# The second product of an MLP, product by product over eight pairs of units, with the sums on VectorE and the squares on ScalarE

## The chip, the cores and the metric

One core of one Trainium2 chip runs the whole program. The metric is the device time of one execution in microseconds (us), lower is better; the median of several runs counts. The engines are named TensorE (PE; PEld is its weight load), VectorE (DVE), ScalarE (ACT), GpSimd (POOL) and SyncE (SP), which issues most transfers.

## The reference, cut to what matters

Two layers over 1024 latent tokens and 256 context tokens of width 1024; layer 0 mixes with windowed attention, layer 1 with gated linear attention. Behind each mixer stands an MLP with 4096 hidden units, in float32:

```python
def channel_mlp(h, w_in, w_out):
    return jnp.square(jax.nn.relu(h @ w_in)) @ w_out

x_lat = x_lat + m_lat[2] * rms_norm(y_lat, g_post_mix[i])
f_lat = channel_mlp(modulate(x_lat, g_pre_mlp[i], m_lat[3], m_lat[4]), w_mlp_in[i], w_mlp_out[i])
x_lat = x_lat + m_lat[5] * rms_norm(f_lat, g_post_mlp[i])
```

The context goes through layer 0's MLP as well and is dropped after layer 1's mixer. The output is the latent stream.

## The kernel before, in words

Tokens are handled in tiles of 128: tiles 0 and 1 are the context, 2 to 5 and 6 to 9 the two halves of the latent tokens. Every float32 product is made from three matmuls: each operand is split into a high part (a cast on ScalarE) and a low part (a subtract on VectorE; both in `split`, L207), and `mm3` (L225) adds high x high, high x low and low x high. Such a triple is the unit of TensorE's work here.

Both products of an MLP use seven products of sums instead of eight (Winograd's form of Strassen's scheme) on quarters: activations by halves of the tokens and of the features, weights by halves of the features and of the columns. The products are numbered 1 to 7 and run in the order 1, 6, 7, 4, 5, 3, 2. Products 1, 6, 7 and 4 run into one bank and 5 and 3 into another; in between, the bank is read and added to an accumulator.

The first product (`mlp_hidden`, L836) walks over 16 pairs of hidden units (a unit is 128 of the 4096). The sums of weight quarters are on GpSimd (L884). A bank goes through ScalarE (copy, rectify) and the square is a GpSimd product (`squared`, L886). The hidden units are stored in DRAM, in layer 0 with layer 1's modulation vectors computed alongside (`mod_sums`).

The second product (`mlp_out`, L981) walks over blocks of pairs of units: sizes 3, 3, 3, 3, 3 in layer 0 and 4, 4, 3, 3 in layer 1. In a block a product is made for one pair of tiles after the other (five pairs in layer 0, the first of them the context's; four in layer 1), with all units of the block in a row for each; then the bank is read (`read`, L997: ScalarE copies the first time, VectorE adds after that, L1004). The sums of weight quarters (L1035) and of hidden quarters (L1078) are on GpSimd. The units that are left, two in layer 0 and four in layer 1, are multiplied as they are, tile by tile (`last_block`, L1143, tile name `py`). There a finished tile goes to `finish`: in layer 0 (`finish0`, L1701) norm, gate (on GpSimd, L1717), residual, norm, transposed modulated input of layer 1, and layer 1's first projection (`gla_v`); in layer 1 (`finish1`, L1836) norm, gate, residual and the store of the output.

What is issued when stands on a written timeline: `tl.at(t, f)` gives each step a nominal time, and `run` issues in the order of these times. The framework then orders each engine's instructions, earlier issued first among those that it deems ready. Loads are issued on SyncE's queue, in order. All large buffers come from one pool of 45 slots of 128 x 1024 floats (`u`; `SLOTS`, L39); a load waits until a slot is free. TensorE's banks are four single ones (`ps1`, L203) and two double ones (`ps2`, L200). The context's products are in half of a double one (`half_bank`).

Of the kernel before, what the change touches and what calls it, by code (L numbers as in the profile page):

```python
# [18 lines left out]
P = 128  # L19
# [24 lines left out]
class Acts:  # L44
    """Activations with the features on the partitions, as high and low parts, by groups of token tiles."""
# [32 lines left out]
class Timeline:  # L78
    """What is to be issued, each at a time of its own on a nominal clock; run() issues in the order of these times."""
# [86 lines left out]
class Backbone:  # L166
    def __init__(self, es, tc, t, out):
        self.tc, self.nc, self.t, self.out = tc, tc.nc, t, out
        self.n = 0
        self.cp = es.enter_context(tc.tile_pool(name="cp", bufs=1))  # L170
# [31 lines left out]

    def ps1(self, s="b"):  # L203
        return self.pp.tile([P, 512], F32, tag="b", name=self.nm(s), bufs=4)

# [5 lines left out]
    def weight(self, srcs, s="w"):  # L211
        """Loads one 128 x 1024 unit of a weight and splits it into a high and a low part."""
# [19 lines left out]
    def rms(self, x, junk):  # L232
        """1 / rms(x), over the features."""
# [12 lines left out]
    def consts(self):  # L246
# [25 lines left out]
        # 32 columns from a feature tile's two on; what comes of the others is never read  # L272
# [45 lines left out]
    def mod_columns(self, l, j, acc):  # L318
        """Columns g * (1 + scale) or shift, for lat (s = 0) and ctx (s = 1)."""
# [3 lines left out]
        for s, a in enumerate(acc):  # L323
            col = out[:, s, :]
            for q in range(2):
                pt = self.ps1("modT")
# [13 lines left out]
    def mod_gate(self, l, which, acc):  # L340
        """gate * g_post, a stream's half of the columns on 32 partitions."""
# [4 lines left out]
        ps = self.ps1("mod")  # L346
# [14 lines left out]
    def mod_first(self):  # L361
        """Layer 0's first shift and scale, one feature tile after the other."""
# [41 lines left out]
    def gate_rows(self, l, which, s):  # L404
        """gate * g_post as a row over all partitions."""
# [3 lines left out]
        for j in range(2):  # L409
            r = 32 * (2 * s + j)  # L410
            pb = self.ps1("grow")
# [5 lines left out]
    def normed(self, x, junk=None):  # L417
        """x (128 tokens x 1024) over its rms; in place where there is another place for the squares."""
# [8 lines left out]
    def modulated(self, xn, l, which, s, dst=(), put=None):  # L427
        """The normed tile, transposed, modulated and split into the pieces of dst, or put where put says."""
        nc = self.nc
        G, S = self.pre[l, which]  # L430
        for q in range(2):
            pt = self.ps1("xt")
# [18 lines left out]
    def post_norm(self, y, x, grow):  # L451
        """x + gate * g_post * rms(y)."""
# [15 lines left out]
    def attn_consts(self):  # L468
# [6 lines left out]
        # by pairs of query heads: pair of kv heads, place within the group, kv head  # L475
# [4 lines left out]
        # keys: previous block | own block | next block | ctx  # L480
# [27 lines left out]
    def first_tiles(self, xs, h, pre):  # L508
        """Modulation, weights and projections of the first two tiles, by feature tile as the loads arrive."""
# [51 lines left out]
    def qkv_out(self, i, pq, pkv):  # L561
        """Rows of q, k and v; the rotary positions on latent tiles."""
# [14 lines left out]
    def keys(self, i):  # L577
        """Transposed keys of a tile as high and low parts, each twice over the partitions: in steps."""
# [36 lines left out]
    def queries(self, qs, i, g):  # L615
        """Transposed queries of a block, of eight heads: high parts on one half of the partitions, low on the other."""
# [48 lines left out]
    def block(self, i):  # L665
        """Keys of a block of 128 queries: latent range, width, mask and key tiles."""
# [11 lines left out]
    def scores(self, i, p, i4, qs):  # L678
        """Probabilities of a pair of query heads (one of each kv head of the pair p)."""
# [43 lines left out]
    def turned(self, i, probs):  # L723
        """The pair's probabilities with the keys on the partitions, by key tile and head."""
# [43 lines left out]
    def attention(self, steps, weights, o_ready):  # L768
        """Pairs of heads in turn: the turning of the probabilities lags the scores, and the values lag that."""
# [7 lines left out]
        for t in range(len(pairs) + LAG_T + 1):  # L777
# [12 lines left out]
            if t < len(pairs) and i4 == 0:  # L790
                # the next unit's queries, and the keys of the tile after the next, in the course of this unit
# [20 lines left out]
    def out_proj(self, o, wo, between):  # L812
        """y (128 tokens x 1024, in PSUM) = o @ w_o; between: what to issue in its midst."""
# [13 lines left out]
    def hidden_store(self, ctx):  # L827
        return [
            (
                self.dp.tile([P, 4, 2, P], F32, name=self.nm("hd")),  # L830
                self.dp.tile([P, 2, P], F32, name=self.nm("hc")) if ctx else None,
            )
            for _ in range(HID // P)
        ]

    def mlp_hidden(self, tl, t0, x, store, g):  # L836
        """Puts the squared rectified hidden units on the timeline, to be stored; the first g pairs of units side by side."""
# [48 lines left out]
        def squared(t, dst):  # L886
            nc.gpsimd.tensor_tensor(dst, t, t, op=ALU.mult)  # L887

        def out(m, a, half, t):
            s = st[m]  # L890
            if ("h", a) not in s:
                s["h", a] = self.u((P, 4, 2, P), s="h")
            squared(t.rearrange("p (i t) -> p i t", i=4), s["h", a][:, :, half, :])
# [1022 lines left out]
```

## Time and profile before

| what | value |
|---|---|
| median of 3 runs | 2704.67 us (2697.41 to 2709.02) |
| profiled execution: own time (its span) | 2705.4 us |
| TensorE matmuls busy | 2590.4 us, 96% |
| VectorE busy | 1881.2 us, 70% |
| GpSimd busy | 1234.1 us, 46% |
| ScalarE busy | 1184.8 us, 44% |
| transfers | 276.30 MB, mean 102 GB/s |

The span is what the profile covers, first instruction to last; nothing of the execution's time lies outside it here. A busy matmul is counted from its start to its modelled end, and matmuls overlap, so TensorE's share is not its share of the best pace. In the span, layer 0's first product runs from 638 us on, its second from 1070, the plain units from 1466; in layer 1 the second product runs from about 2354 to 2698.

### The profile page before, as it was taken

How to read it: one execution, taken by the hardware profiler on the slowest of the kernel's cores; microseconds unless marked ns; L12 is line 12 of the kernel's file. 1: busy time of each engine (PE TensorE's matmuls, PEld its weight loads, DVE VectorE, ACT ScalarE, POOL GpSimd, SP SyncE). 2: the span in 40 equal slices, each digit the busy share in tenths (PEclk: the TensorE clock that was granted, in tenths of full speed). 3: DMA queues.
4: the chain of work that ended last, by engine and by line, in shares of the span. 5: the costliest groups of instructions: out<-in, count | busy, mean ns of one | idle time of the engine just before them, and what ended most of it. 6: DMA issues, size and time to landing. Idle time of an engine off the chain costs nothing.

```text
span 2705.4 us, 36859 instructions
## 1 busy us (share of the span) xinstructions
PE 2590.4 (96%) x13562; PEld 2140.4 (79%) x13562; DVE 1881.2 (70%) x2650; ACT 1184.8 (44%) x2414; POOL 1234.1 (46%) x1287
## 2 busy tenths in 40 slices
PE   7999999998999999999999899999998999999998
PEld 5777888887778888777777788888786888777777
DVE  4788766657877565788996724736648555689886
ACT  3336777645333333533333634434445433454332
POOL 0355655314535456655562512212314656775741
PEclk9999999999999999999999999999999999999999
DMA  9311001321555555322122322002221333531313
GB/s 301 101 55 40 4 2 25 86 86 59 172 165 168 183 180 198 123 105 81 57 87 99 133 54 83 25 23 94 94 95 46 124 110 118 194 140 38 150 71 117
DMA packets 174998, 276.30 MB, mean 102 GB/s; under 512 B 18504, under 2 KB 117088, under 8 KB 174816
## 3 DMA queue, kind: packets, MB, share of 16 engines
q1 hardware_dynamic: 172224, 264.50, 30.0%
q0 software_dynamic: 2592, 9.44, 0.9%
q8 instruction: 107, 1.75, 0.3%
q14 instruction: 75, 0.61, 0.1%
HBM read 214.13 MB, written 59.77 MB: 101 GB/s over the span
## 4 chain that ended last, share of the span: by engine, by line
PE 71%; DVE 18%; issue 4%; ACT 3%; DMA 2%; POOL 2%; SPq 0%; DVEq 0%; POOLq 0%; ACTq 0%
PE p L228 4%; PE p L230 4%; PE p L229 4%; DVE h L209 4%; PE pa L229 3%; PE pa L230 3%; PE pa L228 3%; PE o L756 3%; DVE wu L209 3%; PE pt L737 3%; PE y L230 2%; PE y L228 2%; PE y L229 2%; DVE ma L310 2%; PE rp L230 2%
## 5 line engine op out<-in xcount | busy, mean ns | idle before, releaser
L228 PE MATMUL p<-wu,h 128*128 128x512 f32 x812 | 320.6, 395 | 12.1 <-DVE acc L1004 10.2
L229 PE MATMUL p<-wu,h 128*128 128x512 f32 x812 | 319.0, 393 | 2.8 <-DVE wu L209 2.8
L230 PE MATMUL p<-wu,h 128*128 128x512 f32 x812 | 318.0, 393 | 2.4 <-DVE h L209 2.4
L887 POOL TENSOR_TENSOR h<-s 128x512 f32<-128x512 f32 x128 | 159.7, 1251 | 205.8 <-ACT s L930 188.1
L241 POOL TENSOR_SCALAR rs<-ss 128x1 f32<-128x1 f32 (+1 forms) x81 | 29.3, 361 | 422.5 <-ACT later L235 271.7
L209 DVE TENSOR_TENSOR wi<-wi,wi 128x512 fp32r<-128x512 f32 x176 | 180.5, 1058 | 46.9 <-ACT wi L208 45.9
L310 DVE SCALAR_TENSOR_TENSOR ma<-wm,cT,ma 128x1024 f32<-128x1024 f32 x112 | 166.8, 1521 | 47.1 <-DMA wm<-in_w_mod 46.9
L228 PEld LDWEIGHTS p<-wu,h 128*128 128x128 f32 x812 | 153.8, 189 | 50.6 <-issue 6.2
L1004 DVE TENSOR_TENSOR acc<-acc,p 128x512 f32<-128x512 f32 x220 | 145.7, 678 | 65.6 <-PE p L230 65.4
L230 PEld LDWEIGHTS p<-wu,h 128*128 128x128 f32 x812 | 153.7, 189 | 37.0 <-DVE h L209 4.4
L229 PEld LDWEIGHTS p<-wu,h 128*128 128x128 f32 x812 | 153.8, 189 | 36.2 <-DVE wu L209 3.9
L209 DVE TENSOR_TENSOR wu<-wu,wu 128x512 fp32r<-128x512 f32 x145 | 148.3, 1023 | 13.2 <-ACT wu L208 13.2
L925 ACT COPY s<-pa 128x512 f32<-128x512 f32 x96 | 56.0, 585 | 226.5 <-PE pa L230 217.8
L209 DVE TENSOR_TENSOR h<-hr,h 128x512 fp32r<-128x512 f32 x145 | 150.3, 1037 | 6.5 <-ACT h L208 5.8
L208 ACT CAST h<-hr 128x512 fp32r<-128x512 f32 x145 | 89.9, 620 | 130.6 <-PE p L230 85.7
L704 DVE CUSTOM_DVE_ANT_0 pr<-sc,mask,nsink 128x640 f32<-128x640 f32 (+2 forms) x144 | 108.5, 775 | 42.9 <-PE sc L693 41.0
L721 POOL TENSOR_SCALAR pr<-pr,den 128x640 f32<-128x640 f32 (+2 forms) x160 | 117.7, 749 | 36.5 <-DVE den L719 17.1
L929 DVE TENSOR_TENSOR s<-pc,s 128x512 f32<-128x512 f32 x64 | 43.8, 685 | 125.5 <-ACT s L925 109.5
L709 ACT ACTIVATE pr<-pr,nm 128x640 f32<-128x640 f32 (+2 forms) x160 | 118.5, 742 | 28.2 <-DVE nm L704 25.0
L208 ACT CAST wu<-wu 128x512 fp32r<-128x512 f32 x145 | 89.9, 620 | 90.3 <-PE p L230 75.3
L208 ACT CAST wi<-wi 128x512 fp32r<-128x512 f32 x176 | 102.9, 616 | 49.1 <-DVE ma L310 16.8
L1078 POOL TENSOR_TENSOR hr<-hr 128x512 f32<-128x512 f32 x29 | 40.9, 1423 | 180.2 <-DMA hr<-hd 159.2
(395 smaller groups left out, 7878.6 us busy)
## 6 DMA issues: line engine op xcount, KB each, us to landing
wm<-in_w_mod SPq DMA_DIRECT2D x96, 512.0 KB, 4.7
wi<-in_w_mlp_in SPq DMA_DIRECT2D x64, 512.0 KB, 5.3
hd<-h SPq DMA_DIRECT2D x64, 512.0 KB, 3.3
wu<-in_w_mlp_out SPq DMA_DIRECT2D x64, 512.0 KB, 5.0
hr<-hd SPq DMA_DIRECT2D x64, 512.0 KB, 7.3
x<-in_x SPq DMA_DIRECT2D x16, 512.0 KB, 3.6
wgr<-in_gla_w_in SPq DMA_DIRECT2D x16, 512.0 KB, 4.2
x1d<-xo POOLq DMA_DIRECT2D x10, 512.0 KB, 3.3
```

The costliest lines, as they stand in the source:

```text
L208: self.nc.scalar.copy(hi, src)
L209: self.nc.vector.tensor_tensor(lo, src, hi.bitcast(F32), op=ALU.subtract)
L228: mm(out, a[0], b[0], start=start, stop=False, skip_group_check=onto)
L229: mm(out, a[0], b[1], start=False, stop=False, skip_group_check=onto)
L230: mm(out, a[1], b[0], start=False, stop=stop, skip_group_check=onto)
L310: nc.vector.scalar_tensor_tensor(acc[s], raw, c, acc[s], ALU.mult, ALU.add)
L704: nc.vector.tensor_tensor_reduce(out=like(pr), in0=like(ps[e][:, off:768]), in1=mask, scale=1.0, scalar=self.nsink[:, c0 + e : c0 + e + 1] ...
L709: nc.scalar.activation(pr, pr, AF.Exp, bias=nm[:, e : e + 1], scale=-1.0, accum_out=sums[:, e : e + 1])
L721: nc.gpsimd.tensor_scalar(probs[e], probs[e], den[:, e : e + 1], 0.0, ALU.mult, ALU.add)
L737: nc.tensor.transpose(pt[:, P * j : P * (j + 1)], probs[e][:, P * kt : P * (kt + 1)], self.ident)
L887: nc.gpsimd.tensor_tensor(dst, t, t, op=ALU.mult)
L1004: nc.vector.tensor_add(acc[i][:, cs], acc[i][:, cs], bank)
```

## The change

The second product has two halves of eight pairs of units. In a half, each of the seven products is made unit by unit: for unit pair j, one triple for every pair of tiles, then the next j. So all banks of a product fill at once, and each is read once per product and half. All 32 units go through the seven products; `last_block` is gone. For each product and unit the quarter of the hidden units and that of the weight are loaded side by side into one slot, summed there by VectorE where the product needs sums, and split as one 128 x 1024 operand. The hidden units are stored by halves of the tokens, and the context's by quarters. Nothing of it is on GpSimd but the small steps of the norms. In the first product the square is a ScalarE activation. Layer 0's tiles 1 and 6 to 9 are finished while products 3 and 2 of the second half run, tiles 0 and 2 to 5 at the end; the gate's product is on VectorE. In layer 1, tiles 6 to 9 are finished during product 3, and tiles 2 to 5 by halves of the columns. `split_last` makes the last 4 (5) units of product 2 run pair of tiles by pair of tiles. While `tight` is set, single-bank helpers take a double bank, since all four single ones hold sums.

The diff, without lines that only drop comments:

```diff
+    def bank(self, s):
+        return self.half_bank(s) if self.tight else self.ps1(s)
...
         def squared(t, dst):
-            nc.gpsimd.tensor_tensor(dst, t, t, op=ALU.mult)
+            nc.scalar.activation(dst, t, AF.Square)
...
-    def mlp_out(self, tl, t0, l, pairs, sizes, store, finish, halved=False):
+    def mlp_out(self, tl, t0, l, pairs, store, split_last, done):
...
+        mm = 0.68
+        step = mm * np_
+        order = (1, 6, 7, 4, 5, 3, 2)
+        when, t = {}, t0
+        for kh in range(2):
+            for k in order:
+                for j in range(8):
+                    when[kh, k, j] = t
+                    t += step
...
+        def fetch(kh, k, j):
+            m = 8 * kh + j
+            if k == 6:
+                k3[m], raw[k, m] = unit("k3"), unit("wh")
+                hid(k3[m][:, 0, :], m, 21)
+                wgt(k3[m][:, 1, :], m, 12)
+                hid(raw[k, m][:, 0, :], m, 22)
+                wgt(raw[k, m][:, 1, :], m, 22)
+                return
+            hq, wq = {1: (11, 11), 4: (22, 21), 5: (11, 22), 3: (12, 22), 2: (12, 21)}[k]
+            r = unit("k2" if k == 1 else "wh")
+            hid(r[:, 0, :], m, hq)
+            wgt(r[:, 1, :], m, wq)
...
+        def sums(kh, k, j):
+            m = 8 * kh + j
+            tt = nc.vector.tensor_tensor
+            if k == 6:
+                a, b, r = k2[m], k3[m], raw.pop((k, m))
+                tt(b[:, 0, :], a[:, 0, :], b[:, 0, :], op=ALU.subtract)
+                tt(b[:, 1, :], r[:, 1, :], b[:, 1, :], op=ALU.subtract)
+                tt(a[:, 0, :], r[:, 0, :], b[:, 0, :], op=ALU.subtract)
+                tt(a[:, 1, :], b[:, 1, :], a[:, 1, :], op=ALU.add)
+                return
+            a, r = k2[m], raw[k, m]
+            if k in (4, 5):
+                tt(r[:, 1, :], r[:, 1, :], a[:, 1, :], op=ALU.subtract)
+            if k == 5:
+                tt(r[:, 0, :], a[:, 0, :], r[:, 0, :], op=ALU.add)
+            if k == 3:
+                tt(r[:, 0, :], r[:, 0, :], a[:, 0, :], op=ALU.subtract)
...
+        def apart(kh, k, j):
+            m = 8 * kh + j
+            src = k2[m] if k in (1, 6) else k3[m] if k == 7 else raw[k, m]
+            hi, lo = (self.u((P, 2, 512), F32R, "o" + x) for x in "hl")
+            self.split(src, hi, lo)
+            ops[k, m] = hi, lo
...
+        def product(kh, k, j, p):
+            m = 8 * kh + j
+            chain = 0 if k in (1, 6, 7, 4) else 1 if k in (5, 3) else 2
+            if j == 0 and k in (1, 5, 2):
+                banks[p, chain] = self.half_bank("px") if p in ctx else self.ps1("p")
...
+            onto = k in (6, 7, 4, 3)
+            self.mm3(banks[p, chain], a, (hi[:, 1, :], lo[:, 1, :]), j == 0 and not onto, j == 7, onto)
...
+                    ts = t - 4.5
+                    if k == 6:
+                        ts = when[kh, 1, 0] + (1.35 * j + 0.6) * step
+                    if k != 7:
+                        tl.at((t if k == 1 else ts) - 9, lambda kh=kh, k=k, j=j: fetch(kh, k, j))
+                    if k not in (1, 7, 2):
+                        tl.at(ts, lambda kh=kh, k=k, j=j: sums(kh, k, j))
+                    tl.at(t - 3.6, lambda kh=kh, k=k, j=j: apart(kh, k, j))
+                    for p in range(np_):
+                        tp = t + mm * p
+                        if late:
+                            tp = when[kh, k, 8 - split_last] + mm * (split_last * p + j - 8 + split_last)
+                        tl.at(tp, lambda kh=kh, k=k, j=j, p=p: product(kh, k, j, p))
+                        if j == 7:
+                            tl.at(tp + mm + 0.2, lambda kh=kh, k=k, p=p: read(kh, k, p))
...
-                nc.gpsimd.tensor_tensor(y, y, first["rows"][self.stream(i)], op=ALU.mult)
...
+            nc.vector.tensor_tensor(y, y, first["rows"][self.stream(i)], op=ALU.mult)
...
+        ts, tp, te = self.mlp_out(tl, t1, 0, [(0, 1)] + pairs, store, 4, finish0)
+        early, late = [1] + groups[2], [0] + groups[1]
+        gap = (tp - ts[3] - 22) / 5
+        for n, i in enumerate(early):
+            spots[i] = ts[3] + 5 + gap * n
+        for n, i in enumerate(late):
+            spots[i] = tp + 0.68 * 4 * (n + 1) + 1 + 2.8 * n
...
+        at = te
+        for i in early + late:
+            at = max(at, spots[i] + 12)
+            tl.at(at, lambda i=i: self.gla_v(h2, i, first["wv"], 0))
+            at += 5.45
...
+        self.tight = True
+        ts, tp, te = self.mlp_out(tl, t1, 1, pairs, store, 5, spaced)
+        for n, i in enumerate(groups[2]):
+            spots["whole", i] = ts[3] + 3 + 5.5 * n
...
+        for n, i in enumerate(groups[1]):
+            spots["half", i] = ts[2] + 2 + 2.7 * n
```

The context's quarters are loaded, summed (VectorE) and split once per product and half for all eight pairs, in slots of their own (`cfetch`, `csums`, `capart`), 14, 7 and 4.6 us ahead of the product.

## Rows read from the trace of the kernel before

**Rows 1.** The page's busy time by engine, with share of the span.

```profile
PE 2590.4 (96%) x13562; PEld 2140.4 (79%) x13562; DVE 1881.2 (70%) x2650; ACT 1184.8 (44%) x2414; POOL 1234.1 (46%) x1287
```

**Rows 2.** Timeline of TensorE: start us, duration us, line, tile, shape, count.

```profile
1483.39 1.09 PE L435 MATMUL xt<-ident,xn 128*128 128x128 f32 x8 [0.42 <-DVE xn L1725]
...
2385.03 0.39 PE L228 MATMUL p<-wu,h 128*128 128x512 f32 x1
...
2391.15 0.39 PE L228 MATMUL p<-wu,h 128*128 128x512 f32 x1
```

**Rows 3.** Stages: length, engines' busy us (PE, PEld, DVE, ACT, POOL; counts), clock, DMA, GB/s.

```profile
640.00:860.00 220.00, 201.22 (x1029) 167.77 (x1028) 176.71 (x178) 81.14 (x147) 110.62 (x80) 0.97 0.45 143
...
1070.00:1160.00 90.00, 82.64 (x351) 65.62 (x351) 74.63 (x73) 44.06 (x86) 66.76 (x45) 0.98 0.24 92
1160.00:1466.00 306.00, 293.71 (x1271) 238.64 (x1270) 260.76 (x336) 108.00 (x195) 140.12 (x92) 0.99 0.26 91
1466.00:1565.00 99.00, 90.92 (x415) 72.94 (x415) 69.90 (x112) 53.34 (x124) 50.05 (x50) 0.97 0.29 102
...
2375.00:2480.00 105.00, 98.23 (x408) 79.07 (x407) 94.81 (x96) 48.36 (x91) 76.78 (x48) 0.95 0.23 91
2480.00:2656.00 176.00, 171.28 (x748) 139.73 (x747) 152.34 (x195) 69.48 (x119) 77.11 (x48) 1.00 0.30 111
```

**Rows 4.** TensorE's waits, 1160 to 1466 us, then 640 to 860 us.

```profile
PE px L228 <- DVE acc L1004: 11.0, 4, 2.9
...
PE pc L228 <- DVE s L929: 7.1, 3, 3.6
```

**Rows 5.** Timeline of VectorE around 1170 us, of VectorE and GpSimd around 1221 us.

```profile
1169.18 1.75 DVE L209 TENSOR_TENSOR h<-hr,h 128x512 fp32r<-128x512 f32 x1
1170.86 0.67 DVE L1004 TENSOR_TENSOR acc<-acc,px 128x512 f32<-128x512 f32 x1
...
1220.92 1.75 POOL L1035 TENSOR_TENSOR wu<-wu,wM 128x512 f32<-128x512 f32 x1
...
1221.44 1.78 DVE L209 TENSOR_TENSOR wu<-wu,wu 128x512 fp32r<-128x512 f32 x1
```

**Rows 6.** The instructions of tile wu: duration in ns, min/median/max.

```profile
L209 DVE TENSOR_TENSOR wu<-wu,wu x145: 675/691/1783, 1066.6 to 2625.0; 128x512 fp32r<-128x512 f32 x145
```

**Rows 7.** Timeline of VectorE, back to back, 512 and 1024 wide.

```profile
1174.06 0.68 DVE L209 TENSOR_TENSOR h<-hr,h 128x512 fp32r<-128x512 f32 x1
...
1175.86 0.68 DVE L209 TENSOR_TENSOR h<-hr,h 128x512 fp32r<-128x512 f32 x1
...
2647.18 1.22 DVE L209 TENSOR_TENSOR la<-wu,la 128x1024 fp32r<-128x1024 f32 x1
2648.32 1.22 DVE L209 TENSOR_TENSOR la<-hr,la 128x1024 fp32r<-128x1024 f32 x1
```

**Rows 8.** VectorE's groups by line, 1466 to 1565 us: count, busy us, mean ns.

```profile
L209 DVE TENSOR_TENSOR al<-h,ah 128x256 fp32r<-128x256 f32 (+1 forms) x36 | 18.2, 538 | 2.3 <-ACT ah L208 2.3
L445 DVE TENSOR_SCALAR h<-xt,G,S 128x128 f32<-128x128 f32 x40 | 15.4, 404 | 8.9 <-ACT h L443 8.7
L1711 DVE SCALAR_TENSOR_TENSOR acc<-acc,rs,x 128x1024 f32<-128x1024 f32 x10 | 12.8, 1280 | 3.3 <-POOL rs L242 3.2
...
L1725 DVE TENSOR_SCALAR xn<-acc,rs 128x1024 f32<-128x1024 f32 x10 | 11.1, 1114 | 10.8 <-POOL rs L242 10.8
```

**Rows 9.** GpSimd's and ScalarE's groups by line, 640 to 1070 us.

```profile
L887 POOL TENSOR_TENSOR h<-s 128x512 f32<-128x512 f32 x61 | 73.7, 1209 | 111.6 <-ACT s L930 95.4 <-ACT s L934 15.0 <-DMA hd<-h 0.9
...
L930 ACT ACTIVATE s<-s 128x512 f32<-128x512 f32 x46 | 29.0, 631 | 73.2 <-DVE s L929 73.1
```

**Rows 10.** The same table by stage as in rows 3, first 100 us.

```profile
0.00:100.00 100.00, 85.36 (x585) 66.51 (x586) 55.07 (x105) 39.22 (x69) 13.81 (x32) 0.98 0.72 225
```

**Rows 11.** The page's DMA issues: count, size, median us to landing.

```profile
hr<-hd SPq DMA_DIRECT2D x64, 512.0 KB, 7.3
```

**Rows 12.** The instructions of tile la: duration in ns, min/median/max.

```profile
L208 ACT CAST la<-wu x6: 1047/1050/1059, 1457.3 to 2650.4; 128x1024 fp32r<-128x1024 f32 x6
```

More of the change, by code (lines that the diff above doesn't have):

```diff
@@ L410, in gate_rows @@
             r = 32 * (2 * s + j)
-            pb = self.ps1("grow")
+            pb = self.bank("grow")
             nc.tensor.matmul(pb, self.ident[:, r : r + 1].to_broadcast([P, P]), gm, start=True, stop=True)
@@ L1209, in mlp_out @@
-        t, u0 = t0, 0
-        for nu in sizes:
-            b = Block()
-            b.F, b.S = range(u0, u0 + nu), range(u0 + nu, u0 + 2 * nu)
-            u0 += 2 * nu
-            t = block(b, t)
-        return t, last_block(range(u0, HID // P), t)
+            if (i, c) in seen:
+                nc.vector.tensor_add(acc[i][:, cs], acc[i][:, cs], banks[p, chain])
+            else:
+                seen.add((i, c))
+                nc.scalar.copy(acc[i][:, cs], banks[p, chain])
+            if kh == 1:
+                what = {5: "whole", 3: "half", 2: "whole"}.get(k)
+                if what:
+                    done(what, i, acc[i] if what == "half" else acc.pop(i))
@@ L1218, in gla_consts @@
+        return {k: when[1, k, 0] for k in order}, when[1, 2, 8 - split_last], end
     def gla_consts(self):
@@ L1730, in run, with residual0, residual1 @@
-        self.gla_consts()
-        t2, t3 = self.mlp_out(tl, t1, 0, [(0, 1)] + pairs, (3, 3, 3, 3, 3), store, finish0)
-        first["wv"] = []
-        raws = []
+        def residual0(i, y):
+            rs[i] = self.rms(y, self.junk)
+            nc.vector.tensor_tensor(y, y, first["rows"][self.stream(i)], op=ALU.mult)
+            xn[i] = y
+        def residual1(i):
+            x2 = xn[i]
+            nc.vector.scalar_tensor_tensor(x2, x2, rs.pop(i), x1.pop(i), ALU.mult, ALU.add)
+            if i >= NC_T:
+                nc.sync.dma_start(x2d[i - NC_T], x2)
+            to = self.u(s="xn")
+            rs[i] = self.rms(x2, to)
+            xn[i] = x2, to
@@ new lines, in residual2, with onward, finish0 @@
+        def residual2(i):
+            x2, to = xn[i]
+            nc.vector.tensor_scalar(to, x2, rs.pop(i), None, ALU.mult)
+            xn[i] = to
+        def onward(i):
+            self.modulated(xn.pop(i), 1, 0, self.stream(i), h2.pieces(i))
+        spots = {}
+        def finish0(what, i, y):
+            if what == "half":
+                return
+            t = spots[i]
+            tl.at(t, lambda: residual0(i, y))
+            tl.at(t + 2.5, lambda: residual1(i))
+            tl.at(t + 5, lambda: residual2(i))
+            tl.at(t + 7, lambda: onward(i))
@@ L1740, in run @@
+        tl.at(ts[5] + 2, lambda: next(more))
+        at = te
+        for i in early + late:
+            at = max(at, spots[i] + 12)
+            tl.at(at, lambda i=i: self.gla_v(h2, i, first["wv"], 0))
+            at += 5.45
         tl.run()
-        for i in range(NT, NT + 4):
-            finish0(i, None)
+        self.tight = False
         lat = range(NC_T, NT)
@@ L1834, in load_x3, with scaled, finish1 @@
             nc.sync.dma_start(x, x3d[i - NC_T])
-        def finish1(i, y, n=None):
-            x, row = last["x"][i], last["row"]
-            if n is None:
+        def scaled(i, o, r, halves):
+            for k in range(halves):
+                sl = slice(D // halves * k, D // halves * (k + 1))
+                nc.vector.scalar_tensor_tensor(o[:, sl], o[:, sl], r, last["x"][i][:, sl], ALU.mult, ALU.add)
+                nc.sync.dma_start(self.out[0, P * (i - NC_T) : P * (i - NC_T + 1), sl], o[:, sl])
+        def finish1(what, i, y):
+            row = last["row"]
+            if i in groups[2]:
                 r = self.rms(y, self.junk)
@@ L1842, in finish1 @@
                 nc.vector.tensor_tensor(o, y, row, op=ALU.mult)
[L1843 to L1845 removed]
+                scaled(i, o, r, 1)
                 return
[L1847 to L1848 removed]
+            c = 1 if what == "half" else 0
+            sl = slice(512 * c, 512 * (c + 1))
+            if c:
                 ends[i] = self.u(s="xo"), self.small(2, "ss")
             o, ss = ends[i]
[L1851 removed]
@@ L1852, in finish1 @@
-            if n == 0:
-                nc.gpsimd.tensor_scalar(ss[:, 0:1], ss[:, 0:1], 1.0 / D, EPS, ALU.mult, ALU.add)
-                nc.vector.tensor_tensor(o[:, sl], y[:, sl], row[:, sl], op=ALU.mult)
-                output(i - 1)
+            nc.scalar.activation(self.junk[:, sl], y[:, sl], AF.Square, accum_out=ss[:, c : c + 1])
+            nc.vector.tensor_tensor(o[:, sl], y[:, sl], row[:, sl], op=ALU.mult)
+            if c:
+                nc.gpsimd.tensor_scalar(ss[:, 1:2], ss[:, 1:2], 1.0 / D, EPS, ALU.mult, ALU.add)
@@ L1866, in output @@
-        def output(i):
-            o, r = ends.pop(i)
-            nc.vector.scalar_tensor_tensor(o, o, r, last["x"][i], ALU.mult, ALU.add)
-            nc.sync.dma_start(self.out[0, P * (i - NC_T) : P * (i - NC_T + 1), :], o)
-        t2, t3 = self.mlp_out(tl, t1, 1, pairs, (4, 4, 3, 3), store, finish1, True)
-        tl.at(t2 - 10, last_rows)
-        for n, i in enumerate(lat):
-            tl.at(t2 + (t3 - t2) * n / 8 - 8, lambda i=i: load_x3(i))
+            scaled(i, o, r, 2)
+        spots = {}
```

347 lines of the change are left out of this document (106 added, 241 removed).

## The prediction

> **What bounds the kernel now.** I read the page first: TensorE is busy 96% of the span, no other engine over 70% [rows 1], so a change pays by fewer matmuls or fewer gaps in TensorE's stream. "Busy" hides part of the gaps, so I count matmuls instead. In a dense stretch of the second product the matmul of 512 columns at 2385.03 and the 27th after it at 2391.15 are 6.12 us apart [rows 2]: 0.2267 us each, 0.68 us for a triple (one mm3). The table by stage [rows 3] then gives what each stage lost against that pace:
>
> - layer 0, start of the second product: 90 - 351 x 0.2267 = 10.4 us
> - its middle: 306 - 1271 x 0.2267 = 17.9 us
> - its plain units with the finish of the ten tiles and layer 1's first projection: 415 matmuls, 80 of them transposes at 1.09/8 = 0.14 us [rows 2]; 99 - 335 x 0.2267 - 10.9 = 12.2 us
> - layer 1, start and rest: 105 - 408 x 0.2267 = 12.5, and 176 - 748 x 0.2267 = 6.4 us
>
> Together 59.4 us; that and the matmuls saved are all that the new second product can win. The granted clock is 0.95 to 1.00 in these stages, so the lost time holds some stretches at 1.2 GHz behind each gap.
>
> Why they were lost is seen in the waits and on VectorE. In layer 0's middle the biggest wait is the context's product for a read of its bank, 11.0 us in 4 waits [rows 4]. The timeline shows VectorE late there: a subtract of 1.75 us stands right ahead of that read [rows 5]. The same subtract takes 0.675 us at best, 0.691 in the middle, 1.783 at worst [rows 6], and the long ones run when GpSimd runs a sum: GpSimd from 1220.92 for 1.75 us, VectorE from 1221.44 for 1.78 us, ending 0.55 us after it [rows 5]. So GpSimd's sums hold VectorE up. VectorE is busy 261 of 306 us in that stage and 95 of 105 at layer 1's start [rows 3].
>
> **The change part by part.** The sum is made against the profiled execution's own time, its 2705.4 us span; the median of the three runs, 2704.67 us, is 0.7 us less.
>
> *Matmuls.* Layer 0 had five blocks of three pairs, 5 x 7 x 3 x 5 = 525 triples, and 10 x 2 x 2 = 40 plain ones. It gets 2 x 7 x 8 x 5 = 560. Layer 1 had 14 x 7 x 4 = 392 and 64 plain; it gets 448. 13 triples fewer x 0.68 = 8.8 us less.
>
> *VectorE's load.* Back to back, a 512-wide operation costs 0.60 us (three starts from 1174.06 to 1175.86), a 1024-wide subtract 1.14 us (2647.18 to 2648.32) [rows 7]. A pair of units now needs 7 splits, 1024 wide because hidden and weight quarters lie side by side, and the 8 sums that leave GpSimd: 7 x 1.14 + 8 x 0.60 = 12.8 us. TensorE needs 7 x 2.72 = 19.0 us for it in layer 1 and 7 x 3.40 = 23.8 in layer 0. The reads of banks fall: 2 x 7 x 5 = 70 instead of 175 in layer 0, 56 instead of 112 in layer 1. VectorE gets some 70 to 75% full, without GpSimd in its way. ScalarE's 1024-wide casts are shorter than the subtracts they feed.
>
> *Start and first pass.* While product 1 runs, the four sums for product 6 are due at 1.35 steps a pair: VectorE needs 1.14 + 2.40/1.35 = 2.92 us a step, against 2.72 in layer 1, so it falls 0.2 x 10.8 = 2 us behind by the end; in layer 0 (3.40) it keeps up. In the first half the buffers of the first product's operands are freed only as that ends, so there is no lead. Bounds for each start: nothing, or the 10.4 and 12.5 us lost now. Product 1 needs no sum before it starts, where a block now needs a chain of them, so I take 4 us each, 8 in all, and 2 us more for layer 1's second half.
>
> *Changes of product.* This is the term that the trace shows least. Products now go unit by unit over all pairs of tiles, so the four or five banks of a product end 0.68 us apart instead of 2 us, and the next product wants each again 3 x 0.68 = 2.04 us later in layer 1, 2.72 in layer 0. In between a read of 0.60 us must pass, and VectorE has four or five in a row; queued behind a late read are the next splits and sums, and the next units' matmuls wait for those. There are 28 such changes. From above: the read that came late cost 11.0/4 = 2.8 us each. From below: nothing, if splits run ahead. Layer 1's rest lost 6.4 us over some 16 changes, 0.4 us each, with VectorE at 87% [rows 3]. The new load is nearest to that: 28 x 0.4 = 11 us.
>
> *Layer 0's finish* moves. Before, ten tiles finish at the plain units' pace; now five (1 and 6 to 9) finish while products 3 and 2 run, five behind. From the ten tiles' rows VectorE spends (18.2 + 15.4 + 12.8 + 11.1)/10 = 5.75 us a tile [rows 8], and the product with the gate row comes over from GpSimd at 1.2: 7.0 us; at back-to-back pace 5.6. From the start of product 3 to four units before the end are 12 steps, 40.8 us. VectorE has 13 splits (14.8), 8 sums (4.8), ten reads (6.2), the context's sums and splits (3.4) and five tiles (28 to 35): 57 to 64 us, so it falls 16 to 23 us behind. How much of it reaches TensorE depends on how many splits lie ready: 45 slots less accumulators, layer 1's input and k2 leave a few sets of three. Below nothing is excluded, above it is 23; I take 12, against the 12.2 lost there now. The last five tiles hide under the early tiles' projections. Two gate rows and one modulation vector move with it, onto the wide banks; at a few us of ScalarE they hide under products 5 and 3. *Layer 1's finish*: four tiles 5.5 us apart, each 2.3 us of VectorE on top of 1.14 + 0.6 + 0.3 a step, 3.2 against 2.72 us for eight steps: 4 us. The very end (last matmul, add, square, power, two products, store) is the same work.
>
> *Squares on ScalarE.* GpSimd loses the squares, 61 of 1.21 us in layer 0's first product alone, and the narrower ones of the context; ScalarE does a like activation in 0.631 us [rows 9] and is busy 81 of 220 us there [rows 3], so 38 more hide. GpSimd keeps its weight sums, so VectorE is freed in part. The first stage waits 7.1 us for VectorE's s sums [rows 4] and leaves TensorE idle 18.8 of 220 us [rows 3]. Bounds: 19 us won, 5 lost (ScalarE's copies of a bank now stand behind squares). I take 5 won.
>
> *Transfers.* Each pair now loads 14 quarters of 256 KB, 3.7 MB, for 2.1 MB before. SP issues more, and each queue entry that waits for a slot holds those behind it. In layer 1's first pass product 1's last load is wanted 24.4 us after the first is issued (9 us ahead of the start, to 3.6 ahead of unit 8), and with product 6's loads among them 8 x 0.52 + 5 x 1.05 = 9.4 MB stand ahead: 386 GB/s. The trace's busiest stage moved 225 GB/s at 0.72 of the engines' time [rows 10], 312 at full: 30.2 us, 5.8 late. Loads issued earlier than asked hide this, where slots are free; I price it in the 4 us a start, and as a rival. The Trainium skill, "DMA: Bandwidth & Descriptors", Specifications, gives about 358 GB/s as a core's limit to HBM; by it the 9.4 MB would be an estimated 26.3 us, 1.9 us late, and the change would ask more than the chip gives, but the sum would stay. No row of this kernel comes near either figure.
>
> *Sum.* Lost after: 8 + 2 + 11 + 12 + 4 = 37 us for 59.4 before, 22 us won; with 8.8 and 5: 36 us. 2705.4 - 36 = 2669 us.
>
> **The rivals.** *The changes of product decide (slower).* If every change waits like the context's read now, place: the first matmuls of each product behind the add into acc. 2669 - 11 + 28x: 2705 at x = 1.7 us, 2736 at 2.8. For it: one read more per 0.68 us than VectorE needs with a split between them. Against: layer 1's 0.4 us, measured with inflated subtracts.
>
> *Slots run out in layer 0's finish.* A set of load (7.3 us from a hidden unit's issue to landing [rows 11]), cast 1.05 [rows 12] and subtract 1.2 takes 9.6 us and then 3.4 of use: three sets in flight give 4.3 us a step instead of 3.4, 15 us over 16 steps: 2684; two give 6.5: 2719. For it: twenty slots of layer 1's input and eight of its first weights are claimed there.
>
> *Transfers bound the passes:* 4 x 5.8 = 23 us instead of 10: 2682.
>
> *VectorE is simply free.* No change of product waits, the finishes cost 4, the first products win 10: 2705.4 - 8.8 - (59.4 - 14) - 10 = 2641.
>
> **How the numbers follow.** My forecast 0.45 (2650 to 2688), VectorE free 0.17 (2632 to 2650), transfers 0.10, slots 0.13, changes of product 0.15 (2705 to 2736). The likeliest gives 2669. Both outer cases reach beyond 2632 and 2712; some 0.2 lies outside. About 0.5% (13.5 us) is what a measurement of this kernel tells from no change: faster by more is the first two cases, nearly all of the third and some of the slots', taken a little lower at 0.70; within it 0.16; slower 0.14.
>
> **What the profile would show.** VectorE's subtract 1024 wide at 1.2 us throughout the second product, GpSimd almost empty there; 560 and 448 triples; the lost time by stage 37 us, in starts and layer 0's finish. Wrong if TensorE's waits for acc grow beyond 0.4 us a change, if the load-to-split chain shows in the waits of layer 0's last quarter, if DMA is full in the first pass, or if ScalarE's squares make the first product wait.

## The result, and the profile after

The changed kernel takes 2665.7 us (median of four runs, 2664.2 to 2668.5) against 2703.3 for the kernel before on the same chip: a ratio of 0.9864, 95% interval 0.9846 to 0.9882, or 37.6 us less. The forecast was 2669. The profiled execution took 2665.4 us; its span is 2663.7 us, 41.7 below that of before, which was itself 2.1 us above its median.

The page's busy time by engine answers to [rows 1]; under it is its list of the costliest groups, cut to the two subtracts of the second product (`ol`) and one of the first (`wi`). The columns behind the count are busy us and mean ns of one.

```profile
PE 2565.3 (96%) x13523; PEld 2125.0 (80%) x13523; DVE 1706.7 (64%) x2531; ACT 1258.7 (47%) x2364; POOL 638.5 (24%) x868
...
L214 DVE TENSOR_TENSOR ol<-wh,oh 128x1024 fp32r<-128x1024 f32 x128 | 153.7, 1216 | 54.5 <-ACT oh L213 51.3
L214 DVE TENSOR_TENSOR wi<-wi,wi 128x512 fp32r<-128x512 f32 x176 | 154.7, 910 | 49.5 <-ACT wi L213 47.5
...
L214 DVE TENSOR_TENSOR ol<-k,oh 128x1024 fp32r<-128x1024 f32 x96 | 115.4, 1219 | 26.4 <-ACT oh L213 16.4
```

GpSimd's work is halved, yet VectorE, which took over its sums, is busy 175 us less. The 224 wide subtracts take 1.2 us in the mean, as the prediction had it. The table by stage answers to [rows 3], in the same columns:

```profile
640.00:860.00 220.00, 207.21 (x1077) 174.37 (x1078) 166.06 (x188) 108.80 (x201) 64.70 (x41) 0.98 0.49 150
1068.00:1160.00 92.00, 86.33 (x364) 68.39 (x363) 56.14 (x65) 35.72 (x44) 0.00 (x0) 0.98 0.58 200
1160.00:1400.00 240.00, 238.75 (x1048) 194.77 (x1047) 173.31 (x207) 88.91 (x92) 0.00 (x0) 1.00 0.50 168
1400.00:1466.00 66.00, 55.19 (x235) 43.61 (x234) 54.70 (x76) 35.14 (x62) 13.01 (x20) 0.90 0.56 197
1466.00:1547.00 81.00, 81.00 (x380) 67.04 (x379) 45.95 (x78) 40.25 (x85) 13.54 (x22) 1.00 0.28 90
2330.00:2480.00 150.00, 148.11 (x648) 120.98 (x647) 119.67 (x144) 73.83 (x85) 0.00 (x0) 1.00 0.71 244
2480.00:2655.00 175.00, 171.73 (x749) 141.04 (x747) 129.17 (x155) 62.69 (x75) 16.25 (x18) 0.99 0.49 169
```

By the prediction's count (length less matmuls x 0.2267 us), TensorE lost 92 - 364 x 0.2267 = 9.5 us at layer 0's start, 2.4 in the next 240 us, 150 - 648 x 0.2267 = 3.1 at layer 1's start (its first 12 us still belong to the first product) and 5.2 in its rest. Of the matmuls at 1400 to 1547, 80 are transposes; four of them stand for 0.35 us (in the timeline below, from 1424.61 to 1424.96), so that stage lost 147 - 535 x 0.2267 - 20 x 0.35 = 18.7. Together 38.9 us.

Two places are left, then. At layer 0's start, SyncE's own queue (first of these lines, 1040 to 1105 us) waits for ScalarE's squares, and ScalarE's splits (second, 1040 to 1160 us) wait for loads; the columns are the total, the times and the longest wait:

```profile
SPq L949 <- ACT hx L894: 25.0, 3, 13.1
...
ACT oh L213 <- DMA k<-in_w_mlp_out: 22.4, 6, 6.7
```

L949 stores the context's hidden units. It stands in SyncE's queue ahead of product 1's loads (`k`), so these wait until a square is done. SyncE's timeline shows nothing issued for nearly 8 us ahead of such a store, and the loads right behind it:

```profile
1056.81 0.42 SPq L1024 DMA_DIRECT2D k<-in_w_mlp_out  x1
1064.96 0.79 SPq L949 DMA_DIRECT2D hc<-hx  x2
...
1066.79 0.37 SPq L1019 DMA_DIRECT2D k<-hd  x1
```

The other place is 1400 to 1466. TensorE's timeline shows two of its gaps:

```profile
1424.61 0.60 PE L441 MATMUL xt<-ident,xn 128*128 128x128 f32 x4
1424.96 0.48 PE L234 MATMUL p<-ol,oh 128*128 128x512 f32 x1
...
1428.95 0.60 PE L441 MATMUL xt<-ident,xn 128*128 128x128 f32 x4
1431.92 1.11 PE L441 MATMUL xt<-ident,xn 128*128 128x128 f32 x4 [2.37 <-DVE h L451]
1434.52 0.80 PE L233 MATMUL px<-oh,ch 128*128 128x512 f32 x1 [1.48 <-ACT oh L213]
1435.11 1.91 PE L233 MATMUL p<-oh 128*128 128x512 f32 x4
...
1437.24 0.63 PE L235 MATMUL px<-oh,cl 128*128 128x512 f32 x1
1437.67 0.63 PE L234 MATMUL p<-ol,oh 128*128 128x512 f32 x1
...
1454.76 1.48 PE L233 MATMUL p<-oh 128*128 128x512 f32 x4 [2.50 <-ACT oh L213]
1457.90 0.80 PE L234 MATMUL p<-ol,oh 128*128 128x512 f32 x1 [1.66 <-DVE ol L214]
```

A transpose of a finishing tile waits 2.37 us, in order, for VectorE to empty its bank, the next product 1.48 us for a split, and the matmuls behind them run at half pace, 0.43 us apart (1437.24 to 1437.67). Later two parts of a split are waited for, 2.50 and 1.66 us. The table by stretch has a granted clock of 0.50 at both places, that is 1.2 GHz:

```profile
1431.60:1438.40 6.80, 5.00 (x13) 3.86 (x14) 4.68 (x8) 5.05 (x10) 2.02 (x4) 0.50 0.78 263
...
1455.50:1462.30 6.80, 5.14 (x12) 3.50 (x12) 6.38 (x12) 4.97 (x10) 0.00 (x0) 0.50 1.05 392
```

### The profile page after: what moved, and what is told of

Its sections match the earlier page's. It is cut to its first block, busy times and chain, and to the rows that moved or that the text cites. A ratio compares the mean times of both kernels' runs of the same rounds, so it can differ in the third digit from the quotient of the medians.

```text
span 2663.7 us, 36464 instructions
## 1 busy us (share of the span) xinstructions
PE 2565.3 (96%) x13523; PEld 2125.0 (80%) x13523; DVE 1706.7 (64%) x2531; ACT 1258.7 (47%) x2364; POOL 638.5 (24%) x868
## 5 line engine op out<-in xcount | busy, mean ns | idle before, releaser
L234 PE MATMUL p<-ol,oh 128*128 128x512 f32 x896 | 350.9, 392 | 1.7 <-DVE ol L214 1.7
L235 PE MATMUL p<-oh,ol 128*128 128x512 f32 x896 | 347.1, 391 | 0.0
L233 PE MATMUL p<-oh 128*128 128x512 f32 x896 | 333.0, 394 | 6.7 <-DVE acc L1123 3.7
L233 PEld LDWEIGHTS p<-oh 128*128 128x128 f32 x896 | 170.0, 190 | 44.4 <-ACT oh L213 4.7
L234 PEld LDWEIGHTS p<-ol,oh 128*128 128x128 f32 x896 | 169.6, 189 | 38.8 <-DVE ol L214 2.9
L235 PEld LDWEIGHTS p<-oh,ol 128*128 128x128 f32 x896 | 169.3, 189 | 35.5 <-issue 0.2
L214 DVE TENSOR_TENSOR ol<-wh,oh 128x1024 fp32r<-128x1024 f32 x128 | 153.7, 1216 | 54.5 <-ACT oh L213 51.3
L213 ACT CAST oh<-wh 128x1024 fp32r<-128x1024 f32 x128 | 132.4, 1052 | 107.8 <-PE p L235 45.5
L214 DVE TENSOR_TENSOR ol<-k,oh 128x1024 fp32r<-128x1024 f32 x96 | 115.4, 1219 | 26.4 <-ACT oh L213 16.4
L233 PE MATMUL y<-woh,oh 128*128 128x512 f32 x288 | 114.0, 396 | 0.0
```

The costliest lines, as they stand in the source:

```text
L213: self.nc.scalar.copy(hi, src)
L214: self.nc.vector.tensor_tensor(lo, src, hi.bitcast(F32), op=ALU.subtract)
L233: mm(out, a[0], b[0], start=start, stop=False, skip_group_check=onto)
L234: mm(out, a[0], b[1], start=False, stop=False, skip_group_check=onto)
L235: mm(out, a[1], b[0], start=False, stop=stop, skip_group_check=onto)
```

## The experiments

All ratios are to the kernel before. "After" is the changed kernel.

**GpSimd's lock: what does moving the sums win?** Two experiments, one from each side. In after, the eight sums of a pair go back to GpSimd:

```
-            tt = nc.vector.tensor_tensor
+            tt = nc.gpsimd.tensor_tensor
```

> The changed kernel with the eight sums of a pair of units in the second product on GpSimd instead of VectorE; the walk, the splits and the context's sums stay. Theory (the lost time of the second product came from GpSimd's sums holding VectorE's subtracts up): the 1024-wide subtracts grow from 1.22 us to 1.5 us and more in the mean, late reads come back, TensorE loses 10 to 25 us more in the two second products: 2676 to 2691 us. Rival (the gain is the walk's and the matmuls', VectorE has room for the holds): 2662 to 2670 us, since VectorE has 4.8 us less to do for each pair.

2714.1 us, 1.0040 (1.0024 to 1.0055): 48 us more than after, well past the range, and the whole gain gone. TensorE's biggest waits at 1070 to 1600, then at 2340 to 2710 us, one subtract's duration (ns: min/median/max), and under them the page's lines for both subtracts:

```profile
PE px L233 <- ACT oh L213: 10.5, 6, 3.6
...
PE p L233 <- DVE acc L1123: 12.3, 4, 6.6
...
L214 DVE TENSOR_TENSOR ol<-wh,oh x128: 1210/1226/2361, 1140.5 to 2687.1; 128x1024 fp32r<-128x1024 f32 x128
```
```profile
L214 DVE TENSOR_TENSOR ol<-wh,oh 128x1024 fp32r<-128x1024 f32 x128 | 210.7, 1680 | 79.5 <-ACT oh L213 73.3
L214 DVE TENSOR_TENSOR ol<-k,oh 128x1024 fp32r<-128x1024 f32 x96 | 157.5, 1669 | 108.5 <-ACT oh L213 69.7
```

The longest subtract is 2361 ns; in after it is 1239. The mean goes from 1216 and 1219 to 1680 and 1669 ns, 99 us more of VectorE's time in all. In the trace 104 of the 224 subtracts are over 15% longer than an undisturbed one, and each of the 104 overlaps a two-operand instruction of GpSimd in time; in after none is. So the hold that the prediction read from one pair of rows, here called the lock, is back. But a sum is also slower by itself (on GpSimd 135.10 us for 79 at 1160 to 1400, 1.71 each, for 0.60 back to back on VectorE), so the 48 us are lock and slow sums together, and no run parts them. From the other side, the kernel before keeps its blocks and its plain units, and only its sums and differences move to VectorE:

```
-                nc.gpsimd.tensor_tensor(out, x, y, op=op)
+                nc.vector.tensor_tensor(out, x, y, op=op)
```

(at both places, L1035 and L1078)

> The kernel before with one part alone: the sums of weight and hidden quarters of the second product on VectorE instead of GpSimd; blocks, plain units and squares stay. Theory (GpSimd's hold is what cost): layer 0's middle loses 5 us instead of 17.9 and layer 1's second product some 8 less, total 2680 to 2692 us against 2703. Rival (the walk over eight pairs is what won, by its fewer reads): VectorE has the sums on top of 175 and 112 reads and gets the bound, 2703 us or more.

2654.8 us, 0.9816 (0.9786 to 0.9846): 50 us less than before, and 11 less than after. The theory's number was too small too. Its table by stage:

```profile
1080.00:1160.00 80.00, 80.00 (x355) 66.26 (x354) 68.08 (x113) 43.70 (x84) 3.09 (x3) 1.00 0.27 102
1160.00:1400.00 240.00, 240.00 (x1060) 198.81 (x1059) 220.81 (x372) 86.92 (x162) 0.00 (x0) 1.00 0.28 103
...
2375.00:2480.00 105.00, 105.00 (x464) 86.92 (x464) 97.53 (x161) 44.88 (x82) 0.00 (x0) 1.00 0.33 130
```

TensorE never stops in these three, with VectorE at 92% and 93% in the last two, fuller than before ([rows 3]: 85% and 90%), but without GpSimd beside it. The subtracts `wu<-wu,wu` and `h<-hr,h`, 290 in all, take 690 ns in the mean here, for 1023 and 1037 in before. There 118 of them are long by the same measure, each beside a two-operand instruction of GpSimd; here none is. So the sums' engine made the gain; the walk over eight pairs was not needed for it.

**The squares' engine.** In after, back to GpSimd:

```
-            nc.scalar.activation(dst, t, AF.Square)
+            nc.gpsimd.tensor_tensor(dst, t, t, op=ALU.mult)
```

> The changed kernel with one part undone: the squares of the hidden units are products on GpSimd again. Theory (part of the gain is GpSimd's hold on VectorE in the first product): layer 0's first product loses again the 9 us that TensorE now loses less between 640 and 1060 us, VectorE's subtracts of wi go back from 910 ns to about 1050 ns in the mean, total 2671 to 2676 us against 2665.7. Rival (the squares are worth nothing, all of the gain is in the second product): 2663 to 2669 us, with the longer subtracts hidden.

2674.5 us, 0.9891 (0.9862 to 0.9921): the squares on ScalarE are worth 8.8 us. The first product's stage, 640 to 860 us, and the page's line for its subtract:

```profile
640.00:860.00 220.00, 201.85 (x1030) 168.84 (x1029) 175.14 (x177) 81.16 (x146) 107.45 (x79) 0.96 0.46 142
```
```profile
L214 DVE TENSOR_TENSOR wi<-wi,wi 128x512 fp32r<-128x512 f32 x176 | 179.2, 1051 | 39.4 <-ACT wi L213 38.4
```

That is [rows 3]'s first line again: TensorE idle 18 us, VectorE 9 us busier for 11 fewer instructions than in after. The subtract's mean is 1051 ns again, as expected, for 910 in after: it is the same lock, beside a square that itself takes 1.23 us on GpSimd for 0.63 on ScalarE. Both moves together, on the walk of before (the two edits of before shown above, with `nc.scalar.activation` for the squares):

> The kernel before with the second product's sums on VectorE and the squares on ScalarE; blocks and plain units stay. What then is left to the changed kernel's 2665.7 us is the worth of the walk, of the 13 triples (8.8 us) and of the moved finish. Theory: the two together give what e1 and e3 give apart, 2672 to 2684 us, so that little more than the 8.8 us of matmuls is left. Rival (the walk): 2690 us or more.

2651.15 us, 0.9803 (0.9768 to 0.9838), below both ranges. With the same engines for sums and squares the kernel in blocks beats the changed one by 14.5 us, although it runs 39 matmuls more (8.8 us). What the change brings beside these two moves (the walk, the layout of the stores, the finishes and the gate's engine) is thus a loss in sum; the runs don't split it by part. Some of it lies outside the second product: at the start of layer 1's first product TensorE waits 10.2 us at once for `q`, VectorE's quarter of its input, in after and 3.6 in the blocks (L451 and L445), and no run touched that. The squares are worth only 3.7 us here, inside the spread of the runs.

**Reads of banks at the changes of product.** In after, each read of a bank by VectorE is made twice, the second into a spare tile:

```
+                nc.vector.tensor_tensor(self.half("spare"), acc[i][:, cs],
+                    banks[p, chain], op=ALU.add)
```

> The changed kernel with every VectorE read of a bank done a second time, into a scratch buffer (the result stays). It doubles the suspected cost at the 28 changes of product: four or five reads in a row, each 0.60 us more. Theory (the read of a bank stands between a product's last and the next one's first matmul, with 2.04 us for it in layer 1): 0.6 to 2.4 us more at each change that has reads on VectorE, 12 to 50 us in all, 2678 to 2715 us. Rival (reads have room): at most 4 us more, 2664 to 2670 us.

2713.3 us, 1.0030 (1.0019 to 1.0042): 47.6 us more, the upper end. TensorE's biggest wait at 2340 to 2710 us:

```profile
PE p L233 <- DVE spare L1124: 24.4, 5, 8.0
```

So in layer 1 the changes of product are the place where a fuller VectorE comes out: there the second product takes 28 us longer. In layer 0 they are a part of it only. The middle, 1160 to 1400, runs 56 matmuls fewer (12.7 us), but the biggest wait of layer 0 is again that of the finishing tiles' transposes for VectorE, 17.6 us for 4.3 in after. Taking the changes apart, with the last two units of every product walked pair of tiles by pair of tiles, so that its banks end further apart:

```
-                    late = kh == 1 and k == 2 and j >= 8 - split_last
+                    last = split_last if kh == 1 and k == 2 else 2
+                    late = j >= 8 - last
```

(and `last` for `split_last` in the due times)

> The changed kernel with the last two units of every product run pair of tiles by pair of tiles (as the last four or five of the whole already are), so that banks end 1.36 us apart instead of 0.68, and the next product wants a bank again 0.68 us a pair later. Theory (the changes of product cost, because reads come too fast for VectorE): 4 to 8 us less lost in the middle of layer 0 and in layer 1, 2657 to 2662 us. Rival (what is lost there is late splits, not late reads): 2664 us or more, since two operands must now be ready at once.

2659.0 us, 0.9833 (0.9805 to 0.9860): 6.7 us less than after (2657.1 to 2660.5 for 2664.2 to 2668.5). From 2480 to its last matmul at 2647.0 us TensorE now runs at full pace (739 x 0.2267 = 167.5 us), where after lost 5.2. The 3.1 us by 2480 stay (3.3 here).

**SyncE's queue at layer 0's start.** In after, the stores of hidden units go out on GpSimd's queue:

```
-            nc.sync.dma_start(store[0][2 * m + a], st[m]["h", a])
+            nc.gpsimd.dma_start(store[0][2 * m + a], st[m]["h", a])
```

(and the store of the context's units at L949)

> The changed kernel with the stores of the hidden units issued on GpSimd's queue instead of SyncE's. Theory (the 9.5 us lost at layer 0's start come from loads of product 1 queued on SyncE behind stores of the context's hidden units, which wait 25 us for ScalarE's squares): the loads go out on time, 5 to 9 us won, 2657 to 2661 us. Rival (the loads are late because the first product's operands hold the slots, or because the engines of the transfers are full): 2663 to 2668 us.

2654.9 us, 0.9816 (0.9793 to 0.9839): 10.8 us less than after, a little past the theory's range. Layer 0's start, to be read against after's second line above:

```profile
1068.00:1160.00 92.00, 92.00 (x408) 76.07 (x407) 64.05 (x75) 42.72 (x52) 1.07 (x2) 1.00 0.53 188
```

TensorE never stops. The transfers move no faster (188 GB/s for 200): order in the queue, not the transfers' rate, lost the 9.5 us. The Trainium skill, "SBUF — State Buffer", in its section on the two sides, warns of DMAs issued from GpSimd's queue: some VectorE work locks GpSimd out, and the transfer then looks blocked. That speaks against this edit; no such cost shows in this run.

**Layer 0's finish.** First theory: five tiles are crowded into too short a stretch. Their due times are spread:

```
-        gap = (tp - ts[3] - 22) / 5
+        gap = 5.5
```

> The changed kernel with layer 0's five early tiles finished 5.5 us apart instead of 3.76 us on the nominal clock, so that they spread over most of products 3 and 2. Theory (the 19 us that TensorE loses between 1400 and 1466 us come from five tiles crowded into 20 us: VectorE's and ScalarE's work and the one free double bank for the transposes): 8 to 14 us less is lost there, 2652 to 2658 us. Rival (each tile's transposes wait for their bank whatever the spacing, since the halves share one bank): 2663 to 2669 us.

2666.1 us, 0.9856 (0.9833 to 0.9880): no change. VectorE is 8 us less busy in the stretch and TensorE idles as long (11.9 us for 10.8), now behind a split (second view, its biggest wait at 1400 to 1470):

```profile
1400.00:1466.00 66.00, 54.13 (x222) 42.77 (x221) 46.66 (x63) 31.01 (x53) 11.82 (x20) 0.90 0.53 181
```
```profile
PE px L233 <- ACT oh L213: 9.9, 3, 4.6
```

Second theory: SyncE's queue again. In after it waits 38.0 us in four waits (1390 to 1490 us) for VectorE's residual sums, at the stores of the x2 tiles, ahead of operand loads:

```
-                nc.sync.dma_start(x2d[i - NC_T], x2)
+                nc.gpsimd.dma_start(x2d[i - NC_T], x2)
```

> The kernel after with one line changed: the stores of the residual tiles x2 in layer 0's finish go out on GpSimd's queue, where SyncE's queue stood 38.0 us in four waits for VectorE's residual sums (1390 to 1490). Theory A (the queue: operand loads stand behind those stores): the 19.0 us that TensorE lost at 1400 to 1466 fall to some 8, the waits of the splits for their loads go, and the time is 2653 to 2658. Theory B (the transposes of the finishing tiles and the splits on ScalarE lose them, in order on their engines, and the loads are only late with them): the loads come earlier, TensorE still loses 16 or more, and the time is 2662 to 2667.

2663.1 us, 0.9853 (0.9834 to 0.9872): theory B, no gain to be told from none. SyncE's waits and then the stage:

```profile
SPq L1019 <- PE p L235: 23.3, 6, 6.8
SPq L1645 <- PE px L235: 11.0, 2, 9.6
```
```profile
1400.00:1466.00 66.00, 56.30 (x236) 44.91 (x235) 53.01 (x75) 36.84 (x65) 15.37 (x24) 0.90 0.56 194
```

The store's wait is gone from SyncE's queue, and the loads now wait for TensorE to free their slots instead; one matmul more runs in the stretch. So this long wait on a queue was no loss by itself.

**Put together.** After with the stores, the late pairs and the x2 stores:

> The kernel after with three edits at once: the context's hidden stores on GpSimd's queue, the last two units of every product pair of tiles by pair of tiles, and the x2 stores on GpSimd's queue. Theory A (each loss is a place of its own): the gains add up, 10.8 of the first, 6.7 of the second and 7 to 12 of the third: 2636 to 2641. Theory B (the third gives nothing, and the first two partly overlap, since the late pair of units also gives loads time): 2647 to 2652, no better than the walk by blocks with the same moves of engines.

2650.9 us, 0.9804 (0.9787 to 0.9820): theory B. 14.8 us less than after, where the two that gave something by themselves sum to 17.5; the finish keeps its loss. The same with the due times spread:

> The three edits of the run before last, and the due times of layer 0's early finishing tiles spread to 5.5 us apart instead of the planner's own figure. Theory A (with the queue free, what is left of the finish is work of five engines crowded into too short a stretch): 2 to 6 us below the three edits alone. Theory B (crowding has no part in it, as the same spread alone moved nothing): within 1.5 us of the three edits alone.

2655.0 us, 0.9818 (0.9803 to 0.9833): 4.1 us more than without the spread (2652.6 to 2657.3 for 2649.3 to 2654.1), which neither theory had. The spread gains nothing here either. And the blocks of before with both moves of engines and both kinds of store on GpSimd's queue:

> The walk by blocks of before with its additions and subtractions on VectorE and its squares on ScalarE (2651.15), and now its hidden stores and its x2 stores on GpSimd's queue too. Its TensorE lost nothing at 1080 to 1400, so the hidden stores should give nothing; at 1400 to 1550 it lost about 19, where SyncE's queue stood 47.4 and 22.3 us at the x2 stores for VectorE. Theory A (the queue is the cause in either walk): 2638 to 2645. Theory B (that finish loses to transposes and splits in order, not to loads): 2648 to 2652.

2642.0 us, 0.9770 (0.9755 to 0.9784): the fastest version, 23.7 us below after. The time lies in theory A's range, but its place is another. Blocks with both moves, then the same with the stores moved:

```profile
640.00:1060.00 420.00, 403.94 (x2118) 343.06 (x2117) 267.73 (x312) 202.17 (x377) 109.33 (x69) 0.98 0.53 169
1400.00:1550.00 150.00, 141.53 (x635) 112.52 (x634) 98.56 (x148) 74.50 (x154) 52.20 (x52) 0.98 0.30 93
```
```profile
640.00:1060.00 420.00, 407.05 (x2157) 347.17 (x2156) 278.77 (x324) 205.97 (x383) 138.14 (x130) 0.99 0.54 174
1400.00:1550.00 150.00, 142.91 (x645) 114.39 (x644) 96.43 (x144) 74.18 (x154) 55.02 (x60) 0.98 0.29 83
```

39 matmuls more run in the first product's stage and 10 more in the finish. So the hidden stores did give something, against what was expected, in the first product. In the first of the two SyncE's queue waits 121.0 us for squares at these stores in that stage (75.6 at L941, 45.4 at L938); in the second they are no longer in it. Which waits of TensorE this shortened was not traced to a load, and the runs don't split the two edits.

## Why the prediction was right, step by step

- *Cause.* Right: GpSimd's sums held VectorE up. That the engine of the sums is the cause is shown from both sides, 48 us lost with the sums put back and 50 won with the sums moved alone. That they hold VectorE up is shown by its subtracts, 1680 and 1669 ns in the mean for 1216 and 1219. How much of the gain is this hold and how much the shorter sums stays open. The Trainium skill, "SBUF — State Buffer", section "Who interferes with whom", says that a VectorE instruction with two SBUF inputs contends with a GpSimd instruction that reads SBUF, and that the loser blocks fully. The two in [rows 5] and the subtracts of up to 2361 ns fit.
- *VectorE's load.* Right: some 70 to 75% was expected; it is 72% in layer 0's middle, 80% at layer 1's start and 74% in its rest.
- *Matmuls.* 1008 triples, as predicted (896 of p and 112 of px); -8.8 us.
- *Starts.* Layer 0's was mis-sized: 9.5 us for 4. The step named SP's queue, "each queue entry that waits for a slot holds those behind it", but the entry that held it was a store waiting for a square, and that was not costed, though SyncE's queue waits 25.5 us at 1040 to 1160 us in the trace of before (L941, for GpSimd's squares). Layer 1's start and first pass lost 3.1 us by 2480, for the 6 given them and some of the changes.
- *Changes of product.* Somewhat too high, as a term that could have gone either way: 11 us expected; 2.4 in layer 0's middle and 5.2 in layer 1 behind 2480 measured, where splitting the last two units leaves 1.1 and nothing. Doubling the reads (47.6 us, some of it in layer 0's finish) shows that the rival was not far.
- *Layer 0's finish.* Mis-sized: 18.7 us for 12, inside its bounds of 0 to 23. A reading stands in this: [rows 2] gave 0.14 us for a transpose, from eight that stood behind a wait; in before's dense rows eight take 0.79 us to the next matmul (from 1502.43 to 1503.22), 0.10 each, close to the 0.35 for four in after. At 0.35 before lost some 16 us there, not 12.2. The reason given, VectorE falling behind, fits the chain of waits only in part; less work in the stretch changed nothing, nor did another queue. What the trace shows are transposes and splits waited for in order and stretches of 13.6 us in all at 1.2 GHz behind these gaps. Which of them to mend stays open: banks of their own for the transposes were not tried.
- *Layer 1's finish.* Too high: 4 predicted, and nothing to be seen of it. The 5.2 us lost after 2480 go when the changes of product are taken apart and the finish stays.
- *Squares.* Right in kind, 8.8 us measured for 5, inside the bounds of 5 lost and 19 won; in the kernel in blocks they are worth only 3.7.
- *Transfers.* The rival didn't come: layer 1's start moved 244 GB/s at 0.71 of the engines' time with 3.1 us lost. The 358 GB/s of the Trainium skill, "DMA: Bandwidth & Descriptors", Specifications, weren't reached in any stage of that table. The stretch of 6.8 us from 1455.5 reads 392 GB/s, above that figure, but at a share of 1.05 of the engines' time, so the count over so short a stretch is rough.
- *The sum.* Lost 38.9 us for 37 predicted. That is luck in part: two terms too low (layer 0's start and finish, 12 us) stood beside others too high (changes, layer 1's start and finish, 10 us). The forecast came within 3.3 us of the median; on the span, on which it was made, it is 5.7 too high (2669.4 for 2663.7). Measured from the first product's last matmul, the second products take 31 us less (948.7 us for 965.1 to layer 1's first product, 314.7 for 329.4 to their own end), for 22 + 8.8 predicted; the two first products take 15 us less, for 5. The rest, 4 us, is lost before and after these. What the prediction never asked is what the walk and all that comes with it are worth beside the moves of engines: minus 14.5 us.

## What to carry to other kernels

When a change does several things, price each alone, on the kernel before too: here moving two kinds of work off GpSimd won 53 us and the new walk, with the stores and finishes that came with it, gave back 14.5. A store in an in-order issue queue that waits for compute holds every load behind it; move it to a queue with no loads when the stage behind shows engines waiting for those loads, and not merely because the queue's wait is long (38 us of it were worth nothing here). Count matmuls against the dense pace, not idle time: behind a gap they can run at half the clock and still look busy.

## What was not expected of the hardware

Work on GpSimd beside VectorE costs more than the busy shares tell: with GpSimd busy 46 to 74% of a stage and VectorE 83 to 90% [rows 3], TensorE lost 6 to 12% of it; with VectorE alone at 92 to 93% it lost nothing. Part of this is the lock, which made a subtract of 1.22 us one of 1.67 in the mean, and part the sums' own length on GpSimd. Twice in layer 0's finish the granted clock was 0.50 in the stretch that began about the end of a wait of TensorE, one of 2.37 and one of 2.50 us. And a queue's long wait can be worth 10.8 us or nothing: 25.0 us of waits at L949 the one, 38.0 us at L1656 the other.
